# An embedding gather with positions added: from one stretch of four neighbouring positions per partition to two pairs

## Chip, cores, metric

One core of one Trainium2 chip. The metric is the device time of one execution in microseconds (us). The span of a profile runs from the first to the last instruction record. All runs below were classed "fast"; the clock granted to TensorE was 1.0 in each.

## The reference

```python
batch, seq_len, vocab_size, d_model = 32, 512, 50000, 512
token_embed = embedding_table[indices]            # (32, 512) -> (32, 512, 512) float32
return token_embed + position_embed
```

It reads 16384 random rows of 2 KB (33.5 MB) and writes as much. The additions kept VectorE busy for 87.8 us of the 174.4 in the profile of the kernel before.

## The kernel before

Partition p holds the positions 4p to 4p+3 of a sequence. A slot is one sequence, [128, 4, 512] float32; 23 of them go round. A gather (POOL, an indirect DMA) fetches one row of 2 KB for each partition. VectorE (DVE) adds the position row, and the sync engine (SP) stores two of the four rows at a time.

```python
idx0 = sbuf("idx0", [P, FIRST, 2 * K], i32)          # 128 bytes a partition; the first tile
idx_raw = sbuf("idx_raw", [P, Q * K, 2], i32)
...                                                  # ones, ident, idx_f, idx_t
pos_sb = sbuf("pos_sb", [P, K, D], f32)
slots = [sbuf(f"slot{n}", [P, K, D], f32) for n in range(SLOTS)]
...
out_rows = out.rearrange("b (p k) d -> b p k d", k=K)
...
for g, (b, k) in enumerate(order):                   # POOL: 128 gathers
    if g == half:       nc.gpsimd.wait_ge(s_next, 16)    # indices of sequences 1 to 3
    if g == FIRST * K:  nc.gpsimd.wait_ge(s_idx, J)      # all other indices, transposed
    if b >= SLOTS and k == 0:  ...                       # slot free again
    ins = nc.gpsimd.indirect_dma_start(out=slots[b % SLOTS][:, k, :], ..., in_=table,
        in_offset=bass.IndirectOffsetOnAxis(ap=where, axis=0)).then_inc(s_gather[g % LANES], 16)
    if g >= LANES:
        ins._wait_ge(s_gather[g % LANES], rounds(g - LANES))
...
for adds, b, at, n in stores:                        # SP: 60 half stores, 8 of one row
    nc.sync.dma_start(out=out_rows[b][:, at : at + n, :],
                      in_=slots[b % SLOTS][:, at : at + n, :])._wait_ge(s_add, adds)...
nc.sync.wait_ge(s_rest, 16 * rest)
```

## Time and profile before

| | before |
|---|---|
| timed, 3 runs | 183.49 us (183.45 to 183.49) |
| the profiled execution | 176.13 us, span 174.4 |
| POOL / DVE busy | 121.9 / 89.0 us |
| gathers: first issue, last issue | 2.89, 161.86 us |
| HBM read / written | 34.75 / 33.55 MB |

The lines that carry the reading are in the prediction below. In short, POOL issues a gather each 1.25 us without waiting for anything, and the DMA engines keep up with that pace at 419 GB/s, busy all the while. The profiled execution was 7.4 us shorter than every timed one, and nothing in its profile says why.

### The profile page before, as it was taken

To read this page: it belongs to the slowest core of one execution; us is meant where nothing else is said; L and a number is where in the kernel's file an instruction comes from. 1 tells how busy PE (TensorE), PEld (TensorE's weight loads), DVE (VectorE), ACT (ScalarE), POOL (GpSimd) and SP (SyncE) were. 2 spreads that over 40 slices of the span, in tenths; PEclk is the share of its full clock that TensorE was granted. 3 is DMA by queue.
4 is the path that set the end of the run, shared out by engine and by line. 5 is a ranking of instruction groups with operands and counts; after the bars stand their busy time and mean duration, and the time that the engine had idled before them with its cause. 6 is when DMAs were issued, how large, how long until landed. Compare 5 with 4: busy or idle time off the path is not lost.

```text
span 174.4 us, 427 instructions
## 1 busy us (share of the span) xinstructions
PE 1.0 (1%) x4; PEld 0.4 (0%) x4; DVE 89.0 (51%) x133; ACT 3.6 (2%) x5; POOL 121.9 (70%) x134
## 2 busy tenths in 40 slices
PE   0001100000000000000000000000000000000000
PEld 0000000000000000000000000000000000000000
DVE  0316744745555546455655555555555555555550
ACT  2210000000000000000000000000000000000000
POOL 4777777777777777777777777777777777777200
DMA  3889999999999999999999999999999999999994
GB/s 100 251 260 399 364 385 398 398 396 413 417 418 415 416 420 420 419 420 418 419 420 417 419 421 418 420 419 419 419 418 420 419 419 420 420 417 420 418 413 169
DMA packets 21299, 68.34 MB, mean 392 GB/s; under 512 B 3760, under 2 KB 3888, under 8 KB 21296
## 3 DMA queue, kind: packets, MB, share of 16 engines
q1 hardware_dynamic: 11056, 34.76, 49.6%
q0 software_dynamic: 10240, 33.56, 48.9%
q14 instruction: 3, 0.02, 0.0%
HBM read 34.75 MB, written 33.55 MB: 392 GB/s over the span
## 4 chain that ended last, share of the span: by engine, by line
POOL 65%; issue 22%; DMA 8%; DVE 1%; POOLq 1%; SPq 0%
POOL slot L141 65%; DMA slot<-in_embedding_table_dram,idx_t 4%; DMA slot<-in_embedding_table_dram,idx 3%; DMA idx<-in_indices_dram 1%; DVE idx_t L170 1%; POOLq L149 1%; DVE slot L176 0%; POOLq L136 0%; SPq L221 0%; POOLq L133 0%; SPq L102 0%
## 5 line engine op out<-in xcount | busy, mean ns | idle before, releaser
L141 POOL DMA_INDIRECT slot<-in_embedding_table_dram,idx_t x112 | 105.9, 945 | 34.1 <-issue 34.1
L176 DVE TENSOR_TENSOR slot<-slot,pos_ps 128x512 f32<-128x512 f32 x128 | 87.8, 687 | 80.8 <-DMA slot<-in_embedding_table_dram,idx_t 63.0
L141 POOL DMA_INDIRECT slot<-in_embedding_table_dram,idx x16 | 15.3, 958 | 5.9 <-issue 4.3
L182 ACT COPY pos_ps<-pos_sb 128x512 f32<-128x512 f32 x4 | 2.4, 589 | 8.8 <-DMA pos_sb<-in_position_embed_dram 8.8
L182 ACT ACT_TABLE_LOAD x1 | 1.3, 1283 | 1.0 <-SPq L102 1.0
L170 DVE CAST idx_t<-turned 32x128 int32<-32x128 f32 x4 | 1.1, 280 | 0.1
L154 PE MATMUL turned<-ident,idx_f 128*32 128x128 f32 x4 | 1.0, 416 | 16.9 <-DVE idx_f L164 16.9
L122 POOL MEMSET ones<- 128x128 f32 x1 | 0.2, 204 | 0.5 <-SPq L102 0.5
L154 PEld LDWEIGHTS turned<-ident,idx_f 128*32 128x32 f32 x4 | 0.4, 134 | 17.0 <-DVE idx_f L164 16.9
L123 POOL TENSOR_SCALAR_AFFINE_SELECT ident<-ones 128x128 f32<-128x128 f32 x1 | 0.3, 287 | 0.1
L210 POOL MEMSET const-float32-0.0<- 128x1 f32 x1 | 0.1, 98 | 0.3 <-issue 0.3
L164 DVE CAST idx_f<-idx_raw 128x128 f32<-128x128 int32 x1 | 0.2, 220 | 0.0
L210 POOL MEMSET const-uint8-127<- 128x1 uint8 x1 | 0.1, 115 | 0.0
L210 POOL MEMSET const-bfloat16-1.0<- 128x1 bf16 x1 | 0.1, 109 | 0.0
L210 POOL MEMSET const-float32-1.0<- 128x1 f32 x1 | 0.1, 101 | 0.0
## 6 DMA issues: line engine op xcount, KB each, us to landing
out_dram<-slot SPq DMA_DIRECT2D x60, 512.0 KB, 6.5
out_dram<-slot SPq DMA_DIRECT2D x8, 256.0 KB, 4.8
slot<-in_embedding_table_dram,idx_t POOLq DMA_INDIRECT x112, 7.3
pos_sb<-in_position_embed_dram SPq DMA_DIRECT2D x4, 256.0 KB, 3.9
slot<-in_embedding_table_dram,idx POOLq DMA_INDIRECT x16, 6.0
idx_raw<-in_indices_dram SPq DMA_DIRECT2D x1, 128.0 KB, 3.2
idx<-in_indices_dram SPq DMA_DIRECT2D x1, 4.0 KB, 1.6
idx<-in_indices_dram SPq DMA_DIRECT2D x1, 12.0 KB, 2.6
```

The source lines that it names most:

```text
L122: nc.gpsimd.memset(ones[:], 1.0).then_inc(s_ident, 1)
L123: nc.gpsimd.affine_select(out=ident[:], in_=ones[:], pattern=[[-1, P]], compare_op=mybir.AluOpType.is_equal, fill=0.0, base=0, channel_mul ...
L141: ins = nc.gpsimd.indirect_dma_start(out=slots[b % SLOTS][:, k, :], out_offset=None, in_=table, in_offset=bass.IndirectOffsetOnAxis(ap=whe ...
L149: nc.gpsimd.drain()
L154: ins = nc.tensor.transpose(turned[:, k].rearrange("p b j -> p (b j)"), idx_f[:, :, k], ident[:])
L164: nc.vector.tensor_copy(out=idx_f[:].rearrange("r p k -> r (p k)"), in_=idx_raw[:, :, 0])._wait_ge(s_raw, 16).then_inc(s_cast, 1)
L170: nc.vector.tensor_copy(out=idx_t[j * Q : (j + 1) * Q, :, :], in_=turned[:, :, :, j]).then_inc(s_idx, 1)
L176: nc.vector.tensor_tensor(out=part, in0=part, in1=pos_ps[:, k, :], op=add)._wait_ge(s_gather[g % LANES], rounds(g)).then_inc(s_add, 1)
L182: nc.scalar.copy(out=pos_ps[:, k, :], in_=pos_sb[:, k, :])._wait_ge(s_pos[k], 16).then_inc(s_ps, 1)
L210: nc = _bacc.Bacc("TRN2", target_bir_lowering=False, num_devices=1)
```

## The change

Its intent: partition p holds the positions 2p and 2p+1 of each half sequence, so the two rows that a half store writes lie next to those of the neighbouring partitions, and the store is one contiguous stretch of 512 KB. The positions come in two loads of 512 KB in place of four of 256 KB. The index layout follows: the first index tile holds the first half only, and the transposed indices are wanted from gather 8 on instead of 16.

```diff
-    out_rows = out.rearrange("b (p k) d -> b p k d", k=K)
-    pos_rows = position_embed.rearrange("(p k) d -> p k d", k=K)
+    out_rows = out.rearrange("b (h p r) d -> b h p r d", h=H, r=R)
+    pos_rows = position_embed.rearrange("(h p r) d -> h p r d", h=H, r=R)
...
-    idx0 = sbuf("idx0", [P, FIRST, 2 * K], i32)
-    idx_raw = sbuf("idx_raw", [P, Q * K, 2], i32)
+    idx0 = sbuf("idx0", [P, FIRST, 2 * R], i32)
+    idx_raw = sbuf("idx_raw", [P, Q * R, 2], i32)
...
-        load_pos(nc.sync, 0)
+        load_pos(0)
         nc.sync.dma_start(out=idx0[:, 1:, :], in_=idx_first[:, 1:, :]).then_inc(s_next, 16)
-        load_pos(nc.sync, 1)
         nc.sync.dma_start(out=idx_raw[:], ...).then_inc(s_raw, 16)
-        nc.sync.wait_ge(s_pos[half - 1], 16)
-        load_pos(nc.sync, half)
-        nc.sync.wait_ge(s_gather[0], 16)
-        load_pos(nc.sync, half + 1)
+        nc.sync.wait_ge(s_pos[0], 16)
+        load_pos(1)
...
-            if g == half:
+            if g == R:
                 nc.gpsimd.wait_ge(s_next, 16)
-            if g == FIRST * K:
+            if g == FIRST * R:
                 nc.gpsimd.wait_ge(s_idx, J)
...                                # 2 transposes of 64 columns instead of 4 of 32; casts earlier
-                out=out_rows[b][:, at : at + n, :],
+                out=out_rows[b, at // R][:, at % R : at % R + n, :],
```

More of the change, by code (lines that the diff above doesn't have):

```diff
@@ L12 @@
 FIRST = 4
-Q = 32
+H = 2
+R = 2
+Q = 64
 @with_exitstack
@@ L37 @@
     V, D = embedding_table.shape
-    assert S == P * K and B == 32
+    assert S == P * K and B == 32 and K == H * R
     assert V < (1 << 24), "an index passes through float32"
@@ L43 @@
     idx_words = indices.bitcast(i32)
-    idx_first = idx_words[0:FIRST].rearrange("b (p w) -> p b w", p=P)
-    idx_rows = idx_words.rearrange("b (j w) -> (b j) w", j=J)
-    out_rows = out.rearrange("b (p k) d -> b p k d", k=K)
-    pos_rows = position_embed.rearrange("(p k) d -> p k d", k=K)
+    idx_first = idx_words[0:FIRST, 0:S].rearrange("b (p w) -> p b w", p=P)
+    idx_rows = idx_words.rearrange("b (h j w) -> (b h j) w", h=H, j=J)
+    out_rows = out.rearrange("b (h p r) d -> b h p r d", h=H, r=R)
+    pos_rows = position_embed.rearrange("(h p r) d -> h p r d", h=H, r=R)
     table = embedding_table[:, :]
@@ L57, in psum @@
         return ctx.enter_context(pool).tile(shape, dtype, name=name)
-    idx0 = sbuf("idx0", [P, FIRST, 2 * K], i32)
-    idx_raw = sbuf("idx_raw", [P, Q * K, 2], i32)
+    idx0 = sbuf("idx0", [P, FIRST, 2 * R], i32)
+    idx_raw = sbuf("idx_raw", [P, Q * R, 2], i32)
     ones = sbuf("ones", [P, P], f32)
     ident = sbuf("ident", [P, P], f32)
-    idx_f = sbuf("idx_f", [P, Q, K], f32)
-    idx_t = sbuf("idx_t", [P, K, B], i32)
+    idx_f = sbuf("idx_f", [P, Q, R], f32)
+    idx_t = sbuf("idx_t", [P, R, B * H], i32)
     pos_sb = sbuf("pos_sb", [P, K, D], f32)
     slots = [sbuf(f"slot{n}", [P, K, D], f32) for n in range(SLOTS)]
-    turned = psum("turned", [Q, K, B, J], f32)
+    turned = psum("turned", [Q, R, B * H, J], f32)
     pos_ps = psum("pos_ps", [P, K, D], f32)
-    half = K // 2
-    order = [(b, k) for h in range(2) for b in range(FIRST)
-             for k in range(h * half, (h + 1) * half)]
+    order = [(b, k) for h in range(H) for b in range(FIRST)
+             for k in range(h * R, (h + 1) * R)]
     order += [(b, k) for b in range(FIRST, B) for k in range(K)]
@@ L77 @@
     for g, (b, k) in enumerate(order):
-        if (b <= 1 and k < half) or b == B - 1:
+        if (b <= 1 and k < R) or b == B - 1:
             stores.append((g + 1, b, k, 1))
-        elif k % half == half - 1:
-            stores.append((g + 1, b, k + 1 - half, half))
+        elif k % R == R - 1:
+            stores.append((g + 1, b, k + 1 - R, R))
     sem = tc.alloc_semaphore
     s_first, s_next, s_raw = sem("s_first"), sem("s_next"), sem("s_raw")
-    s_pos = [sem(f"s_pos{k}") for k in range(K)]
+    s_pos = [sem(f"s_pos{h}") for h in range(H)]
     s_gather = [sem(f"s_gather{n}") for n in range(LANES)]
@@ L95, in rounds, with load_pos @@
         return 16 * (g // LANES + 1)
-    def load_pos(engine, k):
-        engine.dma_start(out=pos_sb[:, k, :], in_=pos_rows[:, k, :]).then_inc(
-            s_pos[k], 16
-        )
+    def load_pos(h):
+        nc.sync.dma_start(
+            out=pos_sb[:, h * R : (h + 1) * R, :], in_=pos_rows[h]
+        ).then_inc(s_pos[h], 16)
     with tc.tile_critical(no_gpsimd_drain=True):
@@ L136 @@
                 nc.gpsimd.wait_ge(s_out[b - SLOTS], 16 * done)
-            if b < FIRST:
+            if b < FIRST and k < R:
                 where = idx0[:, b, 2 * k : 2 * k + 1]
             else:
-                where = idx_t[:, k, b : b + 1]
+                at = b * H + k // R
+                where = idx_t[:, k % R, at : at + 1]
             ins = nc.gpsimd.indirect_dma_start(
@@ L152 @@
         nc.tensor.wait_ge(s_ident, 2)
-        for k in range(K):
+        for r in range(R):
             ins = nc.tensor.transpose(
-                turned[:, k].rearrange("p b j -> p (b j)"), idx_f[:, :, k], ident[:]
+                turned[:, r].rearrange("p b j -> p (b j)"), idx_f[:, :, r], ident[:]
             )
             ins.then_inc(s_turn, 1)
-            if k == 0:
+            if r == 0:
                 ins._wait_ge(s_cast, 1)
         for g, (b, k) in enumerate(order):
-            if g == 7:
+            if g == 0:
                 nc.vector.tensor_copy(
-                    out=idx_f[:].rearrange("r p k -> r (p k)"), in_=idx_raw[:, :, 0]
+                    out=idx_f[:].rearrange("q p r -> q (p r)"), in_=idx_raw[:, :, 0]
                 )._wait_ge(s_raw, 16).then_inc(s_cast, 1)
-            if g == 9:
-                nc.vector.wait_ge(s_turn, K)
+            if g == 1:
+                nc.vector.wait_ge(s_turn, R)
                 for j in range(J):
@@ L182 @@
             nc.scalar.copy(out=pos_ps[:, k, :], in_=pos_sb[:, k, :])._wait_ge(
-                s_pos[k], 16
+                s_pos[k // R], 16
             ).then_inc(s_ps, 1)
```

## The prediction

> **What bounds the kernel now.** I read the page first (busy shares, slices, chain), then the waits, the start and the end of the timeline, the chain in order of time at the end, and last the windows.
>
> The page's shares and chain:
>
> ```profile
> PE 1.0 (1%) x4; PEld 0.4 (0%) x4; DVE 89.0 (51%) x133; ACT 3.6 (2%) x5; POOL 121.9 (70%) x134
> ...
> GB/s 100 251 260 399 364 385 398 398 396 413 417 418 415 416 420 420 419 420 418 419 420 417 419 421 418 420 419 419 419 418 420 419 419 420 420 417 420 418 413 169
> ...
> POOL 65%; issue 22%; DMA 8%; DVE 1%; POOLq 1%; SPq 0%
> ```
>
> POOL plus "issue" is 87% of the chain. POOL is only 70% busy because each gather has 0.945 us of busy time and a gap of 0.30 us that waits for nothing. The waits confirm it: no wait of POOL for a landed gather or a freed slot appears at all, and the gaps are all of one size (38.4 us / 126 = 0.305).
>
> ```profile
> POOL slot L141 <- issue: 38.4, 126, 0.3
> POOL slot L141 <- DMA idx<-in_indices_dram: 1.3, 1, 1.3
> ...
> POOL slot L141 <- DVE idx_t L170: 0.3, 1, 0.3
> ```
>
> So POOL issues one gather each 1.25 us from the second one (4.34 us) on, at the same pace when the DMA engines are still nearly empty as later when they are full. First issue 2.89, last 161.86: 127 steps in 158.97 us, 1.252 us each. What follows the last issue is the tail:
>
> ```profile
> 160.61 0.94 POOL slot L141
> 161.56 0.30 issue
> 161.86 7.32 DMA slot<-in_embedding_table_dram,idx_t
> 169.18 0.03 issue
> 169.20 0.69 DVE slot L176
> ```
>
> Then the last single-row store (issued 169.92 and landed 2.9 us later by the trace's semaphore records), and the program's end at 174.4.
>
> The second thing at its limit is the DMA system. One gather of 256 KB (128 rows of 2 KB) and the store of as much each 1.25 us ask for 2 x 262,144 B / 1.252 us = 418.8 GB/s, and the windows show just that flow:
>
> ```profile
> 20.00:40.00 20.00, 0.00 (x0) 0.00 (x0) 10.69 (x18) 0.00 (x0) 15.12 (x17) 1.00 1.01 388
> 40.00:60.00 20.00, 0.00 (x0) 0.00 (x0) 10.82 (x16) 0.00 (x0) 15.13 (x17) 1.00 1.03 416
> 60.00:80.00 20.00, 0.00 (x0) 0.00 (x0) 10.99 (x16) 0.00 (x0) 15.13 (x17) 1.00 1.03 419
> ```
>
> The last two columns are the DMA share and GB/s: the 16 engines always have a packet (1.03). A gather lands about 7.3 us after its issue where the very first one took 3.84, so some 3.5 us of backlog stands in front of each. It is 7.3 at 45 us and 7.3 at 161 us: it neither grows nor drains. POOL's pace and the DMA rate are level within what I can see, and only the gathers' pace and the last landing count for the end.
>
> [...] The trace has 419 sustained, a 4096 B packet taking 159 ns on both queues (16 x 4096 / 159 ns = 412, packets overlapping a little). Stores and gathers cost the same per packet[...]. [...] the indices of sequences 1 to 3, issued at 1.93 us, landed at 1.93 + 2.6 = 4.5, right after the first position load (1.47 + 2.86 = 4.33) that was issued ahead of them, although they are only 12 KB. [...] The 4 KB index load took 1.59 us.
>
> **The change, part by part.**
>
> *Stores.* 60 half stores of 512 KB and 8 single ones of 256 KB stay, with 4096 B and 2048 B packets as before: a partition already held two neighbouring rows, 4 KB contiguous. Only the pitch between partitions falls from 8 KB to 4 KB. At 159 ns a packet, the same as the gathers', I expect no change: 0 us. Sensitivity: stores are half of the DMA work, so 1% cheaper store packets are 0.5% of about 160 us, 0.8 us of DMA time. Since POOL doesn't speed up, cheaper packets can at most drain the backlog in front of the last gather: 7.32 to about 3.84, or 3.5 us. Dearer ones grow it without such a limit.
>
> *Gathers.* 128 of them, 128 rows of 2 KB each, in the same order: 128 x 1.252 us stays.
>
> *Positions.* 4 loads of 256 KB in 2048 B packets become 2 of 512 KB in 4096 B packets. In the packet records a 2048 B packet takes 84 ns in undisturbed stretches: 512 x 84 / 16 = 2.69 us of all engines before, 256 x 159 / 16 = 2.54 after: 0.15 us less DMA work, two issues of some 0.4 us less on SP. None of it is on the path, but it comes earlier: SP no longer waits for the first gather before the last quarter, so the second half is issued at about 5 us instead of 5.79 and 6.75.
>
> *First indices.* 16 B a row instead of 32 B for the first half only; [...] the first gather stays at 2.89 us. The load for sequences 1 to 3 now stands behind 512 KB instead of 256 KB[...]. Each engine has 8 packets of 4096 B in front instead of 8 of 2048 B: 8 x (159 - 84) = 0.6 us later, so landed at 4.5 + 0.6 = 5.1 us (early packets are slower than these, so 5.1 to 5.5). POOL asks for it when the second gather ends, 4.34 + 0.95 = 5.28, and issues at 5.59. Estimated stall: 0 to 0.4 us, in the mean 0.1; it shifts every later gather, so it counts in full.
>
> *The index turn.* Gather 8 (not 16) is now the first that needs the transposed indices: wanted at about 2.89 + 8 x 1.25 = 12.9 us. The raw load lands at about 6 us (6.1 before; less issued ahead of it, a bigger load before it). The cast (0.22) runs before the first add; 2 transposes instead of 4 at 0.42 us; the two casts back (0.28 each) come after the first add, which ends at 6.76 + 0.69 = 7.45 us: done at about 8.1 us, 4.8 us of slack. 2 matmuls and 2 casts fewer are 1.4 us saved on engines that don't bound.
>
> *Tail.* Single stores of the last sequence stay 256 KB in 2 KB packets: 0.
>
> Sum: 0 (gathers) + 0.1 (stall) - 0.2 (a shade less backlog, from the positions' 0.15 and their earlier start) = about -0.1 us. The timed runs are 183.49 and the profiled run is 176.13 with a span of 174.4; the 7.4 us between them lie in nothing that the profile shows. I carry them over unchanged.
>
> **The rivals.**
> - *The contiguous stores speed up HBM.* For it: DMA engines always full, and gather packets average 173 to 182 ns between 10 and 40 us, and some took far longer at 7 to 11 us[...]. Against it: store packets are at 159 ns all along, and POOL sets the pace. Worth at most the 3.5 us of backlog in the profile: 180.0. More only if the unprofiled runs, which are slower, are bound by DMA and not by POOL; their spread of 0.04 us speaks for a fixed pace.
> - *The contiguous stores are worse*[...]. Nothing in the trace speaks for it, but the balance is tight: store packets 2% dearer would be 1.6 us, 185.1.
> - *A start-up stall.* The wait for the indices of sequences 1 to 3 could become up to 1 us if 512 KB take longer at the start (early 2048 B packets show 90 to 136 ns): 184.4. A late index turn would need more than 4.8 us of error; unlikely.
>
> **Range and chances.** The end is fixed by 127 steps of 1.25 us, so neither direction has much room. 183.3 us is the middle; 8 in 10 between 181.9 (part of the backlog drains) and 184.6 (a stall of 1 us). Faster by 2% means under 179.8, more than the whole backlog of the profile: 0.06. Slower by 2% means over 187.2, which needs store packets some 4 to 5% dearer: 0.04. Within: 0.90.
>
> **What would show it.** Right: POOL still shows gaps of 0.3 us only and 1.25 us a gather; the last gather issue is at 161.5 to 162.5 and lands 6.8 to 7.5 us later; 4096 B store packets stay at 159 ns. Right on the start: third gather at 5.6 to 6.0, ninth not later than 13.5, behind no wait for the casts. Wrong: a wait of POOL for the index casts or for landed gathers, a landing time of the gathers that falls towards 4 us (stores became cheaper) or rises through the run (dearer), or timed runs that part from the profiled ones by something else than 7.4 us.

The sum is 0.1 - 0.2 = -0.1 us on the 183.49 timed, with 183.3 named as the middle. The first gather would stay at 2.89 us (0 in the sum); that was the estimate. So was the 0.6 us by which the indices of sequences 1 to 3 would land later: it spreads the 128 packets evenly over the page's 16 engines.

## The result and the profile after

| | before | after |
|---|---|---|
| timed, same rounds | 183.47 us (183.35 to 183.49, 4 runs) | 183.53 us (183.47 to 183.62, 4 runs) |
| profiled execution | 176.13 us, span 174.4 | 183.47 us, span 182.3 |
| first / last gather issued | 2.89 / 161.86 | 3.05 / 161.98 |
| last add begins | 169.20 | 169.85 |
| SP has seen the last store landed | 172.84 | 173.56 |
| from there to the end of the span | 1.58 | 8.71 |

The ratio is 1.0005, 95% interval 0.9988 to 1.0022: same. Ratios here are the mean time of one kernel's fast runs over that of the other's of the same rounds, so not quite the ratio of the medians.

The page of the kernel after:

```profile
span 182.3 us, 418 instructions
...
GB/s 120 236 355 381 345 392 390 390 409 407 418 414 414 409 416 418 414 417 416 417 417 415 417 418 414 417 416 416 417 415 418 415 413 415 411 407 418 352 2 0
...
POOL 63%; issue 24%; DMA 5%; DVE 1%; POOLq 1%; SPq 0%
```

The chain is the same: POOL and its gaps carry it. (Most landing records are missing from this profile, 410 against 3248 before, so that some waits for a DMA show as "issue".) The last two slices, 9 us, have no traffic. What is longer than in the profile of before lies after the work. Up to the last landing the two profiles differ by 0.72 us (172.84 and 173.56).

POOL's waits after (engine, line, releaser: us in total, times, longest):

```profile
POOL slot L141 <- issue: 38.7, 127, 0.3
...
POOL slot L141 <- DMA idx<-in_indices_dram: 1.5, 1, 1.5
```

No wait for the transposed indices and none for sequences 1 to 3: the first wait is the initial index load, the gaps are 127 of 0.3 us. The chain of the start shows the third gather on time (start us, us, what):

```profile
3.05 1.14 POOL slot L141
...
4.50 0.95 POOL slot L141
...
5.75 0.95 POOL slot L141
```

One thing did change. The same long window, first of before, then of after (busy time by engine, then DMA share and GB/s):

```profile
60.00:140.00 80.00, 0.00 (x0) 0.00 (x0) 43.99 (x64) 0.00 (x0) 60.51 (x65) 1.00 1.03 419
```

```profile
60.00:140.00 80.00, 0.00 (x0) 0.00 (x0) 43.67 (x64) 0.00 (x0) 60.50 (x65) 1.00 1.03 416
```

The demand is the same and the engines are as full, yet 3 GB/s less pass. The packet records say where. Between 60 and 160 us, all 10230 packets of 4096 B in the profile of before took 159 ns, on the gathers' queue and on the stores' alike. After, a quarter took longer than 159 ns and 4.5% longer than 165 ns (half of these 168 ns or less, nearly all under 250), and the mean is 160.2. As the gathers are issued at an unchanged pace, the backlog grows: the last add begins 7.87 us after the last gather's issue instead of 7.34.

So three questions were left: where do the 7 us at the end of the after profile come from, do they hide a gain or a loss, and what makes the packets dearer?

### The profile page after: what moved, and what is told of

Its sections match the earlier page's. It is cut to its first block, busy times and chain, and to the rows that moved or that the text cites. A ratio compares the mean times of both kernels' runs of the same rounds, so it can differ in the third digit from the quotient of the medians.

```text
span 182.3 us, 418 instructions
## 1 busy us (share of the span) xinstructions
PE 0.6 (0%) x2; PEld 0.2 (0%) x2; DVE 88.7 (49%) x131; ACT 3.5 (2%) x5; POOL 121.9 (67%) x134
## 4 chain that ended last, share of the span: by engine, by line
POOL 63%; issue 24%; DMA 5%; DVE 1%; POOLq 1%; SPq 0%
POOL slot L141 63%; DMA slot<-in_embedding_table_dram,idx_t 4%; DVE slot L176 1%; DMA idx<-in_indices_dram 1%; POOLq L149 1%; POOLq L135 0%; SPq L221 0%; SPq L104 0%
## 5 line engine op out<-in xcount | busy, mean ns | idle before, releaser
L141 POOL DMA_INDIRECT slot<-in_embedding_table_dram,idx_t x120 | 113.4, 945 | 36.6 <-issue 36.6
L141 POOL DMA_INDIRECT slot<-in_embedding_table_dram,idx x8 | 7.8, 970 | 3.6 <-issue 2.1
L154 PE MATMUL turned<-ident,idx_f 128*64 128x128 f32 x2 | 0.6, 422 | 5.9 <-DVE idx_f L164 5.9
L170 DVE CAST idx_t<-turned 64x128 int32<-64x128 f32 x2 | 0.6, 280 | 0.0
```

Source lines behind the costliest of these rows:

```text
L154: ins = nc.tensor.transpose(turned[:, r].rearrange("p b j -> p (b j)"), idx_f[:, :, r], ident[:])
L170: nc.vector.tensor_copy(out=idx_t[j * Q : (j + 1) * Q, :, :], in_=turned[:, :, :, j]).then_inc(s_idx, 1)
```

## The experiments

"Slow packets" below is the share of 4096 B packets over 165 ns between 60 and 160 us; such a packet carries two gathered rows (in before and after the gathers' queue has 8192 of them for the 16384 rows of 2 KB), or the two rows of one partition in a half store. "Close" is the time from SP's seeing the last landing to the end of the span. Both are from the packet and instruction records of the trace.

| run | chip | median us | before, same rounds | ratio (95%) | slow packets | last gather to last add | close |
|---|---|---|---|---|---|---|---|
| before_again | 6 | 176.36 | 177.12 | 0.996 (0.991-1.000) | 0.1% | 7.44 | 1.57 |
| after_again | 6 | 178.05 | 177.12 | 1.007 (1.002-1.011) | 4.8% | 7.60 | 2.02 |
| half_stores | 6 | 173.68 | 177.12 | 0.982 (0.977-0.986) | (other sizes) | 5.11 | 2.02 |
| act_stores | 6 | 177.18 | 177.12 | 1.002 (0.997-1.007) | 5.2% | 8.54 | 1.29 |
| after_old_pitch | 5 | 183.55 | 183.42 | 1.002 (1.000-1.003) | 3.8% | 8.49 | 8.18 |
| before_new_pitch | 5 | 183.43 | 183.42 | 1.000 (0.999-1.002) | 0.3% | 8.21 | 8.38 |
| pos_four | 5 | 183.47 | 183.42 | 1.000 (0.999-1.002) | 4.2% | 8.61 | 8.35 |
| after_pad | 5 | 183.52 | 183.42 | 1.001 (1.000-1.002) | 5.3% | 8.63 | 8.06 |
| after_realigned | 6 | 176.96 | 176.63 | 1.003 (1.001-1.006) | 0.1% | 7.14 | 2.02 |
| before_shifted | 6 | 177.61 | 176.63 | 1.007 (1.004-1.010) | 6.0% | 8.39 | 1.57 |
| mended | 15 | 183.38 | 183.42 | 1.000 (0.999-1.002) | 0.0% | 7.72 | 8.88 |
| mended_act | 15 | 182.05 | 183.42 | 0.992 (0.991-0.994) | 0.1% | 7.08 | 5.42 |

### 1. Both kernels once more

No edit in either.

> The kernel before, unchanged, for a second profile. Its first profile had a span of 174.4 us beside timed runs of 183.5; the kernel after had 182.3 us. Theory A (the long close of about 8 us on the sync engine, seen after the last store in the profile of after, is in nearly all executions of both kernels, and the first profile of before was the odd one): span 182 us, timed 183.5, and the profile shows slow sync-engine instructions of 0.7 to 1.4 us after the last store landed at about 173 us. Theory B (the close belongs to the changed kernel and the change hides a gain of equal size in the timed runs): span 174 to 176 again.

> The kernel after, unchanged, for a second profile. Theory A: last store landed at 173 to 174 us, a close of 8 to 9 us in most executions, timed 183.5, ratio 0.999 to 1.001. Theory B: the same span but a different ending of the kernel before. Also a measure of how much the start (first gather at 2.89 before, 3.05 after) moves from execution to execution: I expect 0.1 to 0.2 us of it to be noise.

Neither theory, as stated, held. On this chip both kernels close quickly: before at 176.36 us with a close of 1.57 us, after at 178.05 with 2.02. So the close of 8 us is not of the changed kernel (B), and it is not in nearly all executions of both either (A): all timed runs of the two kernels on chip 6 are at 175.9 to 178.6 us, and all on chips 5 and 15 of kernels whose stores SP issues are at 183.3 to 184.3. It goes by chip or session. On a chip with the short close the changed kernel is 0.7% slower, within 2% and clear of 1. That is little more than these rounds can tell: before_again, the very program of before, came out at 0.996.

The ends of the chains, before again and then after again:

```profile
161.88 7.41 DMA slot<-in_embedding_table_dram,idx_t
169.30 0.02 issue
169.32 0.69 DVE slot L176
```

```profile
162.35 7.58 DMA slot<-in_embedding_table_dram,idx_t
169.93 0.02 issue
169.95 0.69 DVE slot L176
```

The spans, 174.7 and 175.9, differ by 1.2 us: 0.05 at the first gather (2.89 and 2.94), 0.42 in POOL's 127 steps, 0.17 in the last gather's landing, 0.14 in the last store and 0.45 in the close. The 0.42 differs between executions of one program: POOL's mean step, from the second gather on and stalls left out, was 1.2494 to 1.2537 us over the fourteen profiles, and 1.2499 and 1.2537 in the two of after. Whether the change makes the high values likelier is not shown: the three of them (1.2527 to 1.2537) fell on kernels with the new layout, of which there are ten profiles, and none on the four profiles built on the kernel before.

### 2. Is it POOL or the DMA engines?

```diff
-    out=out_rows[b, at // R][:, at % R : at % R + n, :], in_=slots[b % SLOTS][:, at : at + n, :]
+    out=out_rows[b, at // R][:, at % R : at % R + 1, :], in_=slots[b % SLOTS][:, at : at + 1, :]
```

> Wrong result on purpose: each half store writes only the first of its two rows (256 KB instead of 512 KB, 2 KB packets); all gathers, adds, waits and issues stay. Store packets of 84 instead of 159 ns are 24% less work for the DMA engines. If POOL's pace sets the time (prediction): gathers still each 1.25 us, last issue at 162 us, landing 3 to 4.5 us later instead of 7.3, so the timed run falls by 2.5 to 4 us, to 179.5 to 181. If the DMA engines set it: 20 to 40 us less.

The window from 60 to 140 us and the end of the chain:

```profile
60.00:140.00 80.00, 0.00 (x0) 0.00 (x0) 43.37 (x66) 0.00 (x0) 60.51 (x65) 1.00 0.96 316
```

```profile
161.95 5.09 DMA slot<-in_embedding_table_dram,idx_t
```

A quarter of the traffic gone (316 GB/s in place of 416), and POOL's last gather is issued at 161.95: POOL sets the pace. Against after_again the time fell by 4.4 us, a little more than the 2.5 to 4 expected. The two profiled spans differ by 4.0: the last landing gave 2.5 of it, the last store 1.1 (2.16 us to be seen landed instead of 3.22), and the earlier issue of the last gather 0.4 (a faster step in this execution). Even with half their bytes gone, then, the stores give back only what lies behind the last gather's issue. One expectation failed: the last landing was to take 3 to 4.5 us and took 5.1, and the DMA share fell only from 1.03 to 0.96. The stores' 2048 B packets took 84 ns as expected, but the gathers' packets took 210 ns in the mean between 60 and 160 us where they took 160 in after. Why is open.

### 3. Who closes?

```diff
-            nc.sync.dma_start(            # stores
+            nc.scalar.dma_start(
...
-        nc.sync.wait_ge(s_rest, 16 * rest)
+        nc.scalar.wait_ge(s_rest, 16 * rest)
```

> Kernel after with all stores and the final wait issued from ACT (idle after its four copies) instead of the sync engine. If the long close hangs on the sync engine having issued the stores or having the final wait: the close shrinks from 9 to about 1.5 us, timed about 176, 4% faster. If the close is the program's own and comes whoever issues the stores: 183.5 within 0.5 us. Gathers' pace unchanged at 1.25 us in both.

It fell on the chip with the short close, so the main question wasn't put. It shows a close of 1.29 us where SP issues no stores; POOL's pace is unchanged (1.25 us a gather, the last at 161.82).

### 4. The stores' addresses

```diff
# after_old_pitch: kernel after, with
-    out_rows = out.rearrange("b (h p r) d -> b h p r d", h=H, r=R)
+    out_rows = out.rearrange("b (p k) d -> b p k d", k=K)
-                out=out_rows[b, at // R][:, at % R : at % R + n, :],
+                out=out_rows[b][:, at : at + n, :],
# before_new_pitch: kernel before, with the reverse
```

> Kernel after with one thing put back: the stores' addresses (4 KB pieces 8 KB apart, as before). Wrong result on purpose: rows land in other places; sizes, counts, waits and order are those of after. In the two profiles of after 3 to 8% of the 4096 B packets take over 165 ns and the flow is 416 GB/s; before 0.0 to 0.1% and 419. Theory S (contiguous stores make packets a little dearer): slow packets fall to 0.0-0.2%, flow 418.5 to 419.5, last gather lands 7.2 to 7.4 us after its issue, time 0.4 to 0.9 us under after. Theory N (chance, or the positions and index loads at the start leave a different backlog): slow packets stay at 3 to 8% and 416 GB/s.

> The reverse: kernel before with the store addresses of after (contiguous 512 KB), nothing else; wrong result on purpose. Theory S: 3 to 8% slow packets, 415.5 to 417 GB/s between 60 and 140 us, last gather 7.5 to 8.3 us, time 1.002 to 1.005 of before. Theory N: as before, ratio 1.000 +- 0.002, no slow packets.

Theory S falls. With the old addresses the kernel after keeps its slow packets (3.8%), and with the new ones the kernel before has 0.3% over 165 ns: 10 between 165 and 250 ns, where the seven profiles with full-sized stores and the tile positions of after (before_shifted, below, among them) have 377 to 596, and 19 over 250. Those 19 did cost something (flow 416 GB/s, landing 8.21), so this one run shows slow packets of a second, rare kind; the three later kernels with contiguous stores and quick packets (after_realigned, mended, mended_act) have 2, 3 and 6 over 250, after_old_pitch with the old stores 11, so I take them for chance and can't prove it. By queue, 28 of the 29 are gather packets: the contiguous store packets themselves average 159.0 ns, as before. What is shown is that contiguity doesn't make the 165 to 250 ns packets. The times of these two runs say little, as both fell on a chip with the long close (section 7).

### 5. Positions, and SP's last instructions

```diff
# pos_four: kernel after, with the four loads of 256 KB and the two waits of SP of before
# after_pad: kernel after, with
         load_pos(1)
+        for _ in range(3):
+            nc.sync.wait_ge(s_pos[0], 16)
```

> Kernel after with the positions in four 256 KB loads and SP's two waits as before. Correct result. Prediction: the position loads are off the path, 0 +- 0.3 us at the start. But the two profiles of after also end 0.43 us later after the last landing (2.01 us instead of 1.58, and SP's first drain takes 129 ns instead of 7, an 8 KB instruction packet comes after and not before it). Theory I [...]: with SP's old number of instructions the close is 1.5 to 1.6 us. Theory L (the close hangs on the loads or stores themselves): it stays at 2.0 us.

> Kernel after with three more waits on SP that are already met, no other change; correct result. Theory I: SP's program has about the length of before again, the close after the last landing is 1.5 to 1.6 us instead of 2.0, so the time falls by about 0.4 us. Theory L: 2.0 us as in after. Slow packets and 416 GB/s as in after in both.

(The 2.01 us in the first of these texts is the close of after's program on chip 6, in after_again and half_stores; the first profile of after closed in 8.71.) Both runs fell on a chip with the long close, so the close as a whole can't be compared; its first step can. From seeing the last landing to the end of SP's first drain, and the time of the last 8 KB packet on the instruction queue (14):

```
run               SP sees landing   drain begins, ns   instruction packet at
before_again          173.12        173.39,   7            172.4
after_again           173.89        174.48, 129            175.1
after_old_pitch       174.16        174.75, 130            175.4
pos_four              173.96        174.23,   7            172.8
after_pad             174.10        174.37,   7            172.9
```

Where SP's program is as long as before (pos_four, or three met waits more), the instruction packet comes before SP wakes and the drain starts 0.27 us after it. Where it is shorter, the packet comes after, and the drain starts 0.59 us after it and is 0.12 longer: 0.44 us together, which is the difference of the closes on chip 6 (1.57 and 2.02). Theory I holds against L: the length of SP's program decides, also with the loads and stores of after (after_pad: 0.27 us and 7 ns). Why it decides is not shown: the packet's time agrees in each run with the drain's, but what the packet carries the trace does not say. The 0.44 us was never timed alone. The position loads themselves are worth nothing that I can see: pos_four has 4.2% slow packets as after has, and its third gather at 5.62 us.

### 6. The slots' alignment

The change halves idx0, the first tile of the program, from 128 to 64 bytes a partition. Every later tile moves down by 64 bytes. By the compiled programs, slot 0 starts at byte 27904 of a partition before, which is 109 x 256, and at 27840 after, which is 192 past a multiple of 256.

```diff
# after_realigned: kernel after, with
-    idx0 = sbuf("idx0", [P, FIRST, 2 * R], i32)
+    idx0 = sbuf("idx0", [P, FIRST, 2 * K], i32)[:, :, 0 : 2 * R]
# before_shifted: kernel before, with 192 unused bytes ahead of the later tiles
+    shift = sbuf("shift", [P, 48], i32)
```

> The store addresses are cleared by the last four runs: the stores of before in the kernel after kept the slow packets, the stores of after in the kernel before had none, and four position loads kept them too. New theory A (alignment): the change halves the index tile idx0 from 128 to 64 bytes a partition, and all later tiles move down by 64 bytes; the slots began at byte 27904 of a partition (109 x 256) before and begin at 27840 (192 past a multiple of 256) after. This is kernel after with idx0 given its old 128 bytes, nothing else; correct result. Theory A: 4096 B packets over 165 ns fall from 3-8% to 0.0-0.3% between 60 and 160 us, flow 419 GB/s instead of 416, last gather 7.2-7.5 us after its issue. Rival G (the gathers' index columns or the turn done earlier leave them slow): 3-8% and 416 stay. In time at most 0.5 us less than after: 177.5 to 178 on a chip with the short close, nothing on one with the long close.

> Kernel before with an unused tile of 192 bytes a partition ahead of the others, so that its slots begin 192 past a multiple of 256 as in after (28096); nothing else, correct result. Theory A: 3-8% slow packets, 415.5 to 417 GB/s, last gather lands 7.6 to 8.5 us after its issue, time 1.002 to 1.005 of before on a chip with the short close. Rival G: none, 419 GB/s, ratio 1.000.

Theory A holds both ways, on one chip. The window from 60 to 140 us of after_realigned, then of before_shifted:

```profile
60.00:140.00 80.00, 0.00 (x0) 0.00 (x0) 43.85 (x65) 0.00 (x0) 60.49 (x65) 1.00 1.03 419
```

```profile
60.00:140.00 80.00, 0.00 (x0) 0.00 (x0) 43.31 (x63) 0.00 (x0) 60.51 (x65) 1.00 1.03 415
```

Realigned, 0.1% of the packets are slow and the flow is 419 GB/s; shifted, the kernel before gets 6.0% and 415. In before_shifted the backlog arrives at the end of the chain:

```profile
161.81 8.36 DMA slot<-in_embedding_table_dram,idx_t
170.17 0.02 issue
170.19 0.69 DVE slot L177
```

8.36 us instead of 7.41 for the last landing, and the whole run 0.7% slower, about 1.2 us, where 0.2 to 0.5% was expected. The gathers' landing grows through the run. From issue to semaphore, the gathers issued at about 43, 78 and 141 us take 7.44, 8.05 and 8.38 us in before_shifted, but 7.43, 7.51 and 7.54 in before_again and 7.29, 7.40 and 7.32 in after_realigned. after_realigned is faster than expected (176.96, not 177.5 to 178) and by its ratio still 0.3% over before; it keeps the late drain (0.59 us after the landing) and had a stall, shown below.

Both rival causes are gone: before_shifted has the old indices, the old turn, the old stores and the old positions. Two things the two runs don't separate. All the later tiles move together, the transposed indices too. That the slots matter is argued from the store packets, which read nothing but slots and are slow as often as the gathers' (4.9 and 7.1% in before_shifted, 4.7 and 4.3% in after). And only starts on a multiple of 256 and 192 past one were tried, so a boundary of 128 bytes would fit as well. How a slot's start makes a packet dearer is not shown. In after the slow packets' median of 168 ns is 5.7% over 159, but three quarters of the misaligned packets still take 159 ns, and the mean is only 0.6 to 0.8% dearer (159.9 to 160.3 ns).

after_realigned also shows the start-up stall of the prediction. POOL's timeline at the start:

```profile
4.37 0.95 POOL L141 DMA_INDIRECT slot<-in_embedding_table_dram,idx  x1 [0.30 <-issue]
5.97 0.94 POOL L141 DMA_INDIRECT slot<-in_embedding_table_dram,idx  x1 [0.65 <-DMA idx<-in_indices_dram]
```

The third gather waited 0.35 us for the indices of sequences 1 to 3. Of the seven profiles in which these stand behind 512 KB of positions, two show such a stall (0.28 us in after_old_pitch, 0.34 beyond the usual step here), five none.

### 7. The change with its flaws out

```diff
# mended: kernel after, with idx0 as in after_realigned, the three waits of after_pad, and
-        load_pos(0)
         nc.sync.dma_start(out=idx0[:, 1:, :], in_=idx_first[:, 1:, :]).then_inc(s_next, 16)
+        load_pos(0)
# mended_act: without the three waits, and with the stores and the last wait on ACT
```

> Kernel after with its three found costs taken out: idx0 at its old 128 bytes (slots on a multiple of 256 again), three met waits more on SP[...], and the indices of sequences 1 to 3 loaded ahead of the first 512 KB of positions (third gather never waits). Correct result. If these three are the whole difference, what is left of the change (contiguous stores, two position loads, turn for 8 gathers earlier) is worth nothing and the kernel equals the one before: ratio 0.998 to 1.002 on any chip; on a chip with the short close median 176.4 to 176.9. If the contiguous stores are worth something that the flaws hid: ratio under 0.997. If another cost is left: over 1.002.

> The same with the stores and the last wait issued from ACT instead of SP, no extra waits. Correct result. The earlier run with ACT stores closed 1.3 us after the last landing where before takes 1.58 and after 2.0. Expected 0.2 to 0.4 us under before on a chip with the short close (ratio 0.998), within noise; on a chip with the long close it tells whether that close of about 8 us belongs to SP having issued the stores (then about 176) or not (183.5).

mended has 0.0% slow packets, 419 GB/s, its third gather at 5.63 us and SP's drain at 173.57, 0.27 after the landing at 173.30, with 7 ns. It equals the kernel before to 0.03% (0.9989 to 1.0016). But this chip has the long close, which blunts the answer:

```
run (long close)    SP sees last landing    end of span
after                    173.56                182.28
after_old_pitch          174.16                182.35
before_new_pitch         173.81                182.19
pos_four                 173.96                182.31
after_pad                174.10                182.16
mended                   173.30                182.18
```

The landings spread over 0.86 us and the ends over 0.19. Whatever ends the program there comes at about 182.2 us whether the work is done at 173.3 or 174.2. In these six profiles several of SP's last instructions take 0.69 to 1.40 us each where the others show 7 to 28 ns, and only 717 to 748 semaphore updates are on record where the short ones have 3718 to 3758. Both belong to the same executions; which is the cause of which, or what a third thing is, no run here shows. It would explain why after and before were equal to 0.05% in the first comparison while after is 0.7% slower on chip 6: in these six profiles, most of a microsecond of lost work is absorbed.

mended_act is the one version with correct results that is clearly under the kernel before in its own rounds: 182.05 us against 183.42, 0.8% less, which is still within 2%; after was not timed in these rounds. SP, freed of the stores, reaches its first closing waits at 170 us, before the work is done, and the close is 5.42 us in place of 8.06 to 8.88. Expected was either 176 or 183.5, so neither: only a part of the close hangs on SP's having issued the stores. On a chip with the short close it was not timed; act_stores, whose slots were misaligned, was within noise of before there.

## Why the prediction was right

The predicted 183.3 us (183.4 by its own sum) and the measured 183.53 agree, and so do the reason for "same" and most steps. That the number came out so close is partly luck, through a thing that the prediction took for a constant.

- **POOL's pace: right.** Last gather at 161.98 us (161.5 to 162.5 said), 1.2514 us a step in the profile of after. half_stores confirms it from the other side: a quarter less traffic doesn't speed up one gather.
- **Stores: right in the term, 0 us.** The swap of addresses in both directions leaves the 165 to 250 ns packets where they were (3.8% over 165 ns in after_old_pitch, 0.3% in before_new_pitch). Contiguous stretches of 512 KB bring nothing measurable here, where the stores' packets have 4096 B either way.
- **"4096 B store packets stay at 159 ns": wrong.** They rose to 160.1 in the mean, and the gathers' packets to 160.2, which the prediction had put down as a sign of dearer stores. By its own sensitivity, 0.8 us for each 1% of the stores, 0.7% on both kinds of packets is an estimate of 1.1 us. The step that failed is the list of what the change adds: it left out that a smaller idx0 moves every later tile by 64 bytes and so takes the slots off their multiple of 256. Realigning took the slow packets away, and shifting the kernel before brought them.
- **"A shade less backlog", -0.2 us: wrong in sign.** The last gather took 7.87 us to its add where 7.34 was seen before (6.8 to 7.5 said for the landing). The alignment is the likely reason, but one last landing is a poor measure: mended, without slow packets, has 7.72, and after_again, with 4.8%, has 7.60. Where the landings are on record, their growth from 43 to 141 us tells the kernels apart: 6.79 to 7.80 in after_again, 7.24 to 7.45 in before.
- **First indices: right.** An estimated stall of 0 to 0.4 us with a mean of 0.1: the seven profiles show 0.28 and 0.34 in two and none in five, a mean of 0.09. The first gather moved by 0.05 and 0.16 us in the two profiles of after. (Its index load took 1.59 us for 4 KB in the profile of before and 1.75 for 2 KB in that of after.)
- **Index turn: right.** The ninth gather was issued at 13.25 us without a wait, under the 13.5 said.
- **Tail, 0 us: incomplete.** It looked at the last store and not at what comes after it. SP's shorter program costs 0.45 us of close on chip 6, with an instruction packet that comes after SP's wake-up.
- **The 7.4 us "carried over unchanged": right as a number, wrong as a picture.** They are not a constant between profile and timing. They are a long close of 8 to 9 us of some chips or sessions (with either close the timed run is 1.2 to 1.8 us longer than its span, 2.8 to 3.6 in mended_act); on chip 6 both kernels time at 176 to 178 us. There the sum is not -0.1 but about +1.2 us (0.7%, interval 0.3 to 2.0 us), at the upper edge of the predicted range, which reaches 1.1 us above before. It is made of the alignment (0.6 us by the ratios of after_again and after_realigned, give or take 0.9; 1.2 by before_shifted, give or take 0.5), the late drain (0.45) and, at times, the stall at the third gather. On chips with the long close most of it seems to vanish in the pinned end, which the prediction did not foresee and which made its number come out to 0.2 us: luck.
- **The rivals.** "Contiguous stores speed up HBM" and "are worse" both fall. "A start-up stall" came as sized. The cost of the alignment was in none of them.

What stays open: the cause of the long close; the rare packets over 250 ns of before_new_pitch; why the length of SP's program moves its first drain; why slots that start 192 past a multiple of 256 have dearer packets, and why only a quarter of these are; and whether mended equals before on a chip with the short close.

## What to carry to other kernels

Before asking what a new layout does for DRAM, look at what the DMA engines move: with the same packets of 4096 B, a contiguous stretch was worth nothing here, and under POOL's issue pace of 1.25 us a gather (1.249 to 1.254 over the fourteen profiles; in before 0.945 busy and a gap of 0.30) a quarter less traffic (half_stores) shortened only the tail: 2.5 us at the last landing and 1.1 at the last store. When a tile changes size, check where the tiles allocated after it now begin; 64 bytes turned 0% slow packets into about 5%, and giving the tile its old size back repaired it. Take a second profile of the kernel before on the same chip before reading a difference between one profile and a timed run as a property of the kernel.
